# RWKV and sparse-attention steps queued behind dense work already written, and one group's element work spread wider

## The chip, the cores and the metric

One core of a Trainium2 chip runs one launch of the kernel. The metric is the device time of the launch in microseconds (us); lower is better. The engines named below are TensorE (PE in the rows; PEld is its weight load), VectorE (DVE), ScalarE (ACT), GpSimd (POOL) and SyncE (SP), which here issues most transfers.

## The reference

One decoder layer on 256 tokens of width 2048, cut to what matters:

```python
p = rms_norm(h) @ w_in                       # all input projections
y_rwkv = rwkv7_group(p[:, :RWKV_COLS])       # 16 heads x 64
#   per token: sa = S @ -kk;  S = S*w + sa (kk*a)^T + v k^T;  y = S @ r
y_att = dsa_group(p[:, RWKV_COLS:])          # indexer scores, top 64 keys of a query, attention
h = h + concat(y_rwkv, y_att) @ w_mix_out
h = h + cross_attention(rms_norm(h), rms_norm(mem))
h = h + square(relu(rms_norm(h) @ w_up)) @ w_down
return rms_norm(h)
```

## The kernel before

**Dense work.** Every large product is written as three matmuls: a float32 weight tile `raw` is loaded (`stream`, L176, SyncE's queue, four buffers), ScalarE copies it to a rounded part `whi` (L182), VectorE subtracts that from it and leaves the rest `wlo` (L183; three buffers of each), and `gemm` multiplies hi by hi, hi by lo and lo by hi: L210 to L212 in a panel of kind "B" (128x256 outputs), L222 to L224 in one of kind "A" (128x512 and 128x296), L216 and L218 in one of kind "C". I write att0#3 for the fourth weight tile of the panel whose weights are `w_att0`. The dense panels of the mixed part come in this order: a small panel, rkv0, gates, rkv1, att1 (attention keys and values), att0 (indexer queries), rkv2 and rkv3 (keys and values of RWKV group 1), ck (cross-attention keys, from `mem`), att2 (attention queries), and then mix0, mix2 and mix1, the output projection of RWKV group 0, of the attention and of RWKV group 1. From 542 us of the span on come only the rest of mix1, cross attention with its projections, and the MLP. An operand tile `xhl` of `mem` is made by `load_t` (ScalarE L311, VectorE L312), and ck's first matmuls need the first of these.

**Side work.** Beside the dense panels go three generators.
- RWKV, once for each of two groups of eight heads. `rwkv_elem` makes two arrays, AR and BK, out of r, k, the decay and the gate, for two pairs of heads at a time: matmuls L453, L468, L490, transposes L509, and on VectorE L471 to L500, L511 to L515, L519 and, last, L518. `rwkv_gram` multiplies them (L538, in four chunks of 64 tokens; L541 masks the result on VectorE), transposes BK and v (L567, L579, L588), and solves a triangular system by a substitution on VectorE (L601, L603), whose result comes back through DRAM (L617) for L631 and L639. `rwkv_state` walks the four chunks (L682 to L702), with outputs L713 and L716 and a normalisation (`norm`: L725 to L747; L740 spreads the scale with a matmul, L743 to L745 and L747 are its tail on VectorE).
- Sparse attention. `dsa_qi` and `dsa_kv` make rotary embeddings and indexer scores (L858, on VectorE L865 and L867) and find the 64 largest by eight rounds of L878 and L879; `dsa_att` is the attention.
- `shift_bank` (L347, L349, L351) mixes an RWKV projection with its neighbour in time, behind each rkv panel.

**What sets the order.** `run` merges the generators: each yields how much dense time its step should be spread over, and `run` always takes the one that is least far (`scaled` multiplies these amounts). A scheduler then works through the operations, and among those that it holds ready, what was written first goes first; it sets the order on each engine for good. On the chip each engine executes its list in that order. The two halves that matter below are `g_stream`, the dense panels, and the others: `r_group(0)`, `r_group(1)` and `d_stream`.

Of the kernel before, what the change touches and what calls it, by code (L numbers as in the profile page):

```python
# [10 lines left out]
F32 = mybir.dt.float32  # L11
# [11 lines left out]
T = 256  # L23
# [56 lines left out]
def hybrid_block(ctx: ExitStack, tc: tile.TileContext, I, out):  # L80
# [36 lines left out]

    done, now = {}, [0.0]

# [3 lines left out]
    def run(*gens):  # L123


        live = [[0.0, g, None, f] for g, f in gens]
        while live:
            ready = [e for e in live if e[2] is None or e[2] in done]
# [7 lines left out]
            try:  # L136
                r = next(e[1])
            except StopIteration:
# [35 lines left out]
    def stream(pack, i, n, hl=None):  # L174
        raw = wpool.tile([P, 1024], F32, tag="raw", bufs=NRAW, name="raw")
        last_load[:] = [nc.sync.dma_start(raw[:, :n], pack[i][:, :n])]  # L176
        if hl is None:
            hi = wop.tile([P, 1024], F32R, tag="whi", bufs=NHL, name="whi")
            lo = wop.tile([P, 1024], F32R, tag="wlo", bufs=NHL, name="wlo")
        else:  # L180
            hi, lo = hl[:, 0], hl[:, 1]
        S.activation(hi[:, :n], raw[:, :n], AF.Copy)  # L182
        V.tensor_tensor(lo[:, :n], raw[:, :n], hi[:, :n].bitcast(F32), op=ALU.subtract)  # L183
        return hi, lo

    def gemm(pack, ncol, kts, xt, blocks, nk=1, hook=None, alt=False):
# [9 lines left out]
        for chunk, k in enumerate(range(0, kts, nk)):  # L196
# [4 lines left out]
            for kind, col, w, bank, sel in blocks:  # L201
                for a in range(n):
                    first, last = k + a == 0, k + a == kts - 1
                    c0 = a * ncol + col
                    wh, wl = hi[:, c0:c0 + w], lo[:, c0:c0 + w]
                    xh, xl = operand(xt, k + a)
                    if kind == "B":
# [3 lines left out]
                        TE.matmul(o, wh, xl, start=False, stop=False, skip_group_check=True)  # L211
                        TE.matmul(o, wl, xh, start=False, stop=last, skip_group_check=True)  # L212
                    elif kind == "C":
# [3 lines left out]
                                  start=first, stop=False, skip_group_check=True)  # L217
                        TE.matmul(o[:, :T], wl, xh, start=False, stop=last, skip_group_check=True)  # L218
                    else:
# [3 lines left out]
                        TE.matmul(o, xh, wl, start=False, stop=False)  # L223
                        TE.matmul(o, xl, wh, start=False, stop=last)  # L224
            yield sum(b[2] if b[0] == "A" else T for b in blocks) * n * 3 * 0.000422
# [790 lines left out]
    def r_group(g):  # L1016
        yield f"r{g}"
        yield (10.0, 10.0)[g]
        yield from scaled(rwkv_elem(g), (0.8, 1.0)[g])
        yield from scaled(rwkv_gram(g), (0.8, 0.75)[g])  # L1020
# [293 lines left out]
```

## Time and profile before

| | us |
|---|---|
| three runs | 1352.95, 1354.51, 1358.34 |
| median | 1354.51 |
| the profiled execution | 1358.12 |
| its span, first to last instruction | 1356.3 |
| TensorE busy / VectorE busy / ScalarE busy in the span | 1318.3 / 876.3 / 684.2 |
| mean granted clock of TensorE (1.0 is 2.4 GHz) | 0.981 |

The rows further down are read in this order: busy shares, the chain that ended last, what TensorE waited for, then windows of the span with busy time and granted clock, and in the windows where clock or busy time fall short the single instructions. In a row of the timeline "[3.17 <-DVE BK L518]" says that the engine stood idle for 3.17 us before it and that the end of L518 on VectorE, writing BK, released it. A clock of 0.5 is TensorE's lower level, 1.2 GHz.

### The profile page before, as it was taken

The numbers are of one execution on the slowest core, as the hardware profiler recorded it, in microseconds if no ns is written. First come the engines' busy times: TensorE is split into PE (matmuls) and PEld (weight loads), VectorE is DVE, ScalarE is ACT, GpSimd is POOL, SyncE is SP. The second block draws the span as 40 slices with busy tenths as digits, with TensorE's granted clock in tenths as the row PEclk, the third lists the DMA queues.
The fourth block names the chain that finished last, engine by engine and source line by source line (L and its number), as shares of the span: only waits on it lengthen the run. The fifth ranks groups of instructions, "written<-read, shape, count | busy, mean of one in ns | idle before, by whom it ended". The sixth has DMA issues, their size and how long they took to land.

```text
span 1356.3 us, 20607 instructions
## 1 busy us (share of the span) xinstructions
PE 1318.3 (97%) x7989; PEld 1141.1 (84%) x7989; DVE 876.3 (65%) x1459; ACT 684.2 (50%) x1009; POOL 20.6 (2%) x69
## 2 busy tenths in 40 slices
PE   7999799997999999999999999999999999999997
PEld 7999788987978778887888888888888888888886
DVE  5477676599777765776665656555656556565655
ACT  5545334546544663666553544445445344363453
POOL 0001000001000000000000000000000000000000
PEclk9999699998899999999999999999999999999999
DMA  8844345334657425565666666666666666666663
GB/s 262 284 133 139 99 156 160 107 109 131 201 153 235 129 83 153 183 219 173 184 186 199 189 190 195 189 190 192 191 190 191 195 187 187 199 188 191 195 190 123
DMA packets 81489, 239.06 MB, mean 176 GB/s; under 512 B 20752, under 2 KB 20880, under 8 KB 81392
## 3 DMA queue, kind: packets, MB, share of 16 engines
q1 hardware_dynamic: 76864, 237.15, 57.4%
q8 instruction: 62, 1.02, 0.3%
q10 hardware_dynamic: 4528, 0.61, 0.3%
q14 instruction: 35, 0.29, 0.1%
HBM read 234.58 MB, written 3.15 MB: 175 GB/s over the span
## 4 chain that ended last, share of the span: by engine, by line
PE 85%; DMA 5%; DVE 5%; ACT 3%; issue 1%; SPq 0%; DVEq 0%; ACTq 0%; POOL 0%; POOLq 0%
PE gb L216 17%; PE gb L222 13%; PE gb L223 13%; PE gb L224 13%; PE gb L218 9%; PE gb L211 4%; PE gb L210 4%; PE gb L212 4%; DVE wlo L183 2%; ACT whi L182 1%; DMA x_tm<-in_x 1%; PE pg L538 1%; PE psi L858 1%; DMA raw<-in_w_mix 1%; DMA x_tm<-in_mem 1%
## 5 line engine op out<-in xcount | busy, mean ns | idle before, releaser
L183 DVE TENSOR_TENSOR wlo<-raw,whi 128x1024 fp32r<-128x1024 f32 (+2 forms) x416 | 498.4, 1200 | 365.5 <-ACT whi L182 362.5
L182 ACT ACTIVATE whi<-raw 128x1024 fp32r<-128x1024 f32 (+2 forms) x416 | 432.1, 1041 | 493.0 <-PE gb L224 249.5
L216 PE MATMUL gb<-xhl,whi 128*128 128x512 f32 x1024 | 350.4, 394 | 0.3 <-DVE hres L1045 0.3
L218 PE MATMUL gb<-xhl,wlo 128*128 128x256 f32 x1024 | 269.9, 279 | 0.0
L216 PEld LDWEIGHTS gb<-xhl,whi 128*128 128x128 f32 x1024 | 189.4, 188 | 38.5 <-ACT xhl L265 0.7
L218 PEld LDWEIGHTS gb<-xhl,wlo 128*128 128x128 f32 x1024 | 192.7, 188 | 6.4
L224 PE MATMUL gb<-whi,ul 128*128 128x512 f32 x480 | 186.9, 389 | 0.0
L223 PE MATMUL gb<-wlo,uh 128*128 128x512 f32 x480 | 186.9, 389 | 0.0
L210 PE MATMUL gb<-xhl,whi 128*128 128x256 f32 x560 | 163.5, 294 | 7.6 <-ACT whi L182 6.2
L211 PE MATMUL gb<-xhl,whi 128*128 128x256 f32 x560 | 163.1, 292 | 0.0
L212 PE MATMUL gb<-xhl,wlo 128*128 128x256 f32 x560 | 160.2, 291 | 2.2 <-DVE wlo L183 2.2
L222 PE MATMUL gb<-whi,uh 128*128 128x512 f32 x480 | 132.2, 389 | 0.0
L210 PEld LDWEIGHTS gb<-xhl,whi 128*128 128x128 f32 x560 | 109.8, 196 | 10.7 <-ACT whi L182 6.2
L212 PEld LDWEIGHTS gb<-xhl,wlo 128*128 128x128 f32 x560 | 109.0, 197 | 4.3 <-DVE wlo L183 2.8
L211 PEld LDWEIGHTS gb<-xhl,whi 128*128 128x128 f32 x560 | 110.2, 197 | 1.7 <-DVE xhl L312 0.9
L222 PEld LDWEIGHTS gb<-whi,uh 128*128 128x128 f32 x480 | 90.1, 188 | 18.8
L224 PEld LDWEIGHTS gb<-whi,ul 128*128 128x128 f32 x480 | 90.1, 188 | 18.7
L223 PEld LDWEIGHTS gb<-wlo,uh 128*128 128x128 f32 x480 | 90.1, 188 | 18.6
L223 PE MATMUL gb<-wlo,xhl 128*128 128x512 f32 (+1 forms) x224 | 82.5, 373 | 0.7 <-DVE wlo L183 0.6
L224 PE MATMUL gb<-whi,xhl 128*128 128x512 f32 (+1 forms) x224 | 81.9, 370 | 0.0
L222 PE MATMUL gb<-whi,xhl 128*128 128x512 f32 (+1 forms) x224 | 65.1, 376 | 0.2 <-ACT whi L182 0.2
L1045 DVE TENSOR_TENSOR hres<-hres,gb 128x512 f32<-128x512 f32 x92 | 57.4, 680 | 0.1
(390 smaller groups left out, 1425.7 us busy)
## 6 DMA issues: line engine op xcount, KB each, us to landing
raw<-in_w_up SPq DMA_DIRECT2D x128, 512.0 KB, 4.2
raw<-in_w_dn SPq DMA_DIRECT2D x128, 512.0 KB, 4.2
raw<-in_w_rkv SPq DMA_DIRECT2D x48, 512.0 KB, 3.9
raw<-in_w_att SPq DMA_DIRECT2D x32, 512.0 KB, 4.2
raw<-in_w_mix SPq DMA_DIRECT2D x32, 512.0 KB, 3.7
raw<-in_w_att SPq DMA_DIRECT2D x16, 296.0 KB, 3.1
rawx<-in_memT SPq DMA_DIRECT2D x8, 512.0 KB, 3.9
raw<-in_w_ck SPq DMA_DIRECT2D x8, 512.0 KB, 3.7
```

Of the source, the lines that this page charges most:

```text
L182: S.activation(hi[:, :n], raw[:, :n], AF.Copy)
L183: V.tensor_tensor(lo[:, :n], raw[:, :n], hi[:, :n].bitcast(F32), op=ALU.subtract)
L210: TE.matmul(o, wh, xh, start=st_, stop=False, skip_group_check=True)
L211: TE.matmul(o, wh, xl, start=False, stop=False, skip_group_check=True)
L212: TE.matmul(o, wl, xh, start=False, stop=last, skip_group_check=True)
L216: TE.matmul(o, wh, xt[(k + a) // 4][:, (k + a) % 4].rearrange("p s t -> p (s t)"), start=first, stop=False, skip_group_check=True)
L218: TE.matmul(o[:, :T], wl, xh, start=False, stop=last, skip_group_check=True)
L222: TE.matmul(o, xh, wh, start=first, stop=False)
L223: TE.matmul(o, xh, wl, start=False, stop=False)
L224: TE.matmul(o, xl, wh, start=False, stop=last)
L538: TE.matmul(pgs[e][:, j * P:j * P + P], BK[half[e], c, j].rearrange("p a t -> p (a t)"), AR[half[e], c, j].rearrange("p a t -> p (a t)"), ...
L1045: V.tensor_tensor(dst, dst, banks[b * 2 + t], op=ALU.add)
```

## The change

`run` traces every step of a generator that is not the first (so all side work) inside `behind(last["mm"])` and `behind(last["lo"])`. `behind` puts a lower bound on the order: TensorE's operations of that step come behind the dense matmul that was written last, VectorE's behind the last `wlo` split that was written. `stream` and `gemm` record these two. Nothing is bound on ScalarE, GpSimd and SyncE. The steps of `rwkv_elem(0)` yield 2.0 instead of 0.8 times their amount, so that group 0's element work, and what follows it, is merged later. `mm_chain` is defined and not called. The number of instructions stays the same on every engine, but for two ACT_TABLE_LOADs fewer on ScalarE. Lines behind the middle of the file move by 16 (L538 is L554 in the new file, L740 is L756, L183 is L199, L210 to L212 are L226 to L228, L222 to L224 are L238 to L240).

```diff
--- before.py
+++ after.py
@@ -1,5 +1,5 @@
 import math
-from contextlib import ExitStack
+from contextlib import ExitStack, nullcontext
 
 import numpy as np
 
@@ -115,7 +115,20 @@
         return pss.tile([P, 512], F32, tag="d", bufs=2, name=name)
 
 
-    done, now = {}, [0.0]
+    def behind(ins):
+
+        return tc.issue_after(ins.ins) if ins else nullcontext()
+
+    def mm_chain(calls):
+
+        prev = None
+        for a, kw in calls:
+            with behind(prev):
+                prev = TE.matmul(*a, **kw)
+
+
+
+    done, now, last = {}, [0.0], {}
 
     def mark(key):
         done[key] = now[0]
@@ -124,6 +137,7 @@
 
 
         live = [[0.0, g, None, f] for g, f in gens]
+        gen0 = gens[0][0]
         while live:
             ready = [e for e in live if e[2] is None or e[2] in done]
             assert ready, [e[2] for e in live]
@@ -134,7 +148,9 @@
             e = min(ready, key=lambda e: e[0])
             now[0] = e[0]
             try:
-                r = next(e[1])
+
+                with behind(e[1] is not gen0 and last.get("mm")), behind(e[1] is not gen0 and last.get("lo")):
+                    r = next(e[1])
             except StopIteration:
                 live.remove(e)
                 continue
@@ -179,8 +195,8 @@
             lo = wop.tile([P, 1024], F32R, tag="wlo", bufs=NHL, name="wlo")
         else:
             hi, lo = hl[:, 0], hl[:, 1]
-        S.activation(hi[:, :n], raw[:, :n], AF.Copy)
-        V.tensor_tensor(lo[:, :n], raw[:, :n], hi[:, :n].bitcast(F32), op=ALU.subtract)
+        last["hi"] = S.activation(hi[:, :n], raw[:, :n], AF.Copy)
+        last["lo"] = V.tensor_tensor(lo[:, :n], raw[:, :n], hi[:, :n].bitcast(F32), op=ALU.subtract)
         return hi, lo
 
     def gemm(pack, ncol, kts, xt, blocks, nk=1, hook=None, alt=False):
@@ -200,7 +216,7 @@
                 hook[k]()
             for kind, col, w, bank, sel in blocks:
                 for a in range(n):
-                    first, last = k + a == 0, k + a == kts - 1
+                    first, end = k + a == 0, k + a == kts - 1
                     c0 = a * ncol + col
                     wh, wl = hi[:, c0:c0 + w], lo[:, c0:c0 + w]
                     xh, xl = operand(xt, k + a)
@@ -209,19 +225,19 @@
                         st_ = first and sel == 0
                         TE.matmul(o, wh, xh, start=st_, stop=False, skip_group_check=True)
                         TE.matmul(o, wh, xl, start=False, stop=False, skip_group_check=True)
-                        TE.matmul(o, wl, xh, start=False, stop=last, skip_group_check=True)
+                        last["mm"] = TE.matmul(o, wl, xh, start=False, stop=end, skip_group_check=True)
                     elif kind == "C":
 
                         o = banks[bank]
                         TE.matmul(o, wh, xt[(k + a) // 4][:, (k + a) % 4].rearrange("p s t -> p (s t)"),
                                   start=first, stop=False, skip_group_check=True)
-                        TE.matmul(o[:, :T], wl, xh, start=False, stop=last, skip_group_check=True)
+                        TE.matmul(o[:, :T], wl, xh, start=False, stop=end, skip_group_check=True)
                     else:
                         o = banks[bank][:, :w]
                         xh, xl = xh[:, sel * P:sel * P + P], xl[:, sel * P:sel * P + P]
                         TE.matmul(o, xh, wh, start=first, stop=False)
                         TE.matmul(o, xh, wl, start=False, stop=False)
-                        TE.matmul(o, xl, wh, start=False, stop=last)
+                        last["mm"] = TE.matmul(o, xl, wh, start=False, stop=end)
             yield sum(b[2] if b[0] == "A" else T for b in blocks) * n * 3 * 0.000422
         return banks
 
@@ -1016,7 +1032,7 @@
     def r_group(g):
         yield f"r{g}"
         yield (10.0, 10.0)[g]
-        yield from scaled(rwkv_elem(g), (0.8, 1.0)[g])
+        yield from scaled(rwkv_elem(g), (2.0, 1.0)[g])
         yield from scaled(rwkv_gram(g), (0.8, 0.75)[g])
         yield from scaled(rwkv_state(g, yr), (0.6, 1.617)[g])
         mark(f"y{g}")
```

The order is the same as before on every engine up to att1#9, and again from the fourth weight tile of mix1 to the end. What happens between is seen at three places.

TensorE, where att1 ends and att0 begins; pg is a product of `rwkv_gram(0)`, gb are dense banks. Before:

```order
L224 MATMUL gb_1433<-whi,xhl 128x296
L538 MATMUL pg_1373<-AR,BK 128x128 x4
...
L538 MATMUL pg_1513<-AR,BK 128x128 x4
L567 MATMUL pb<-par,BK 128x128 x16
L579 MATMUL rb<-par,rke 128x128 x8
L588 MATMUL pv<-par,vp 128x128 x12
L222 MATMUL gb_1923<-whi,xhl 128x512
```

After:

```order
L240 MATMUL gb_1335<-whi,xhl 128x296
L525 MATMUL ss<-par,inve 128x128 x2
L554 MATMUL pg_1692<-AR,BK 128x128 x4
L554 MATMUL pg_1693<-AR,BK 128x128 x4
L238 MATMUL gb_1727<-whi,xhl 128x512
...
L240 MATMUL gb_1730<-whi,xhl 128x512
L554 MATMUL pg_1749<-AR,BK 128x128
...
L583 MATMUL pb<-par,BK 128x128 x8
...
L595 MATMUL rb<-par,rke 128x128 x8
```

The block of 68 products and transposes that stood between the two panels is spread in groups of eight and more over att0; the first eight products and two transposes (L525) still stand between the panels.

TensorE, where rkv3 (bank gb_3383) ends and ck (gb_3838, gb_3839) begins; py, pm, pvv and psdb are RWKV state 0, psi is the indexer, zw, za, sst and ss are `rwkv_elem(1)`. Before:

```order
L211 MATMUL gb_3383<-xhl,whi 128x256
L212 MATMUL gb_3383<-xhl,wlo 128x256
L509 MATMUL ss<-par,inve 128x128 x4
L210 MATMUL gb_3838<-xhl,whi 128x256
L210 MATMUL gb_3839<-xhl,whi 128x256
L453 MATMUL zw<-lx,lora 128x256 x2
L453 MATMUL za<-lx,lora 128x256 x2
L211 MATMUL gb_3838<-xhl,whi 128x256
```

After:

```order
L228 MATMUL gb_3383<-xhl,wlo 128x256
L756 MATMUL psdb<-par,sde 128x128 x2
L729 MATMUL py<-AR,Sn 64x64 x8
L732 MATMUL py<-Gm_1691,X 64x64 x8
L874 MATMUL psi<-kT,qiT 128x256 x4
L741 MATMUL pm<-y,par 128x256
...
L469 MATMUL zw<-lx,lora 128x256 x2
...
L506 MATMUL sst<-par,rkk 128x2 x2
...
L226 MATMUL gb_3838<-xhl,whi 128x256
L226 MATMUL gb_3839<-xhl,whi 128x256
L469 MATMUL zw<-lx,lora 128x256 x2
L227 MATMUL gb_3838<-xhl,whi 128x256
```

Forty-five side matmuls now follow each other between the two panels; 39 of them ran inside rkv2 and rkv3 before.

VectorE in the same place, from one split of ck's weights to the first operand tile of `mem` (xhl). After, with 49 rows left out of the middle; the next split of ck comes 15 rows behind the last one shown:

```order
L199 TENSOR_TENSOR wlo<-raw,whi 128x1024
L883 SCALAR_TENSOR_TENSOR acc<-rel,wi,acc 128x256
L759 TENSOR_TENSOR y<-y,psdb 128x256
...
L534 TENSOR_TENSOR BK<-a__3548,ss 64x4x64 x2
L894 MAX m_3437<-wk 128x8
L328 SCALAR_TENSOR_TENSOR xhl<-rawx,par,xhl 128x256
L534 TENSOR_TENSOR BK<-a__3554,ss 64x4x64 x2
L328 SCALAR_TENSOR_TENSOR xhl<-rawx,par,xhl 128x256 x2
```

Before, the corresponding piece, from the split of the same weight tile (ck#2) on:

```order
L183 TENSOR_TENSOR wlo<-raw,whi 128x1024
L515 SCALAR_TENSOR_TENSOR a__3548<-kx,hkk,a__3548 128x256
L515 SCALAR_TENSOR_TENSOR a__3554<-kx,hkk,a__3554 128x256
L879 MATCH_REPLACE wk<-m_3437,wk 128x256
L518 TENSOR_TENSOR BK<-a__3548,ss 64x4x64 x2
L518 TENSOR_TENSOR BK<-a__3554,ss 64x4x64 x2
L312 SCALAR_TENSOR_TENSOR xhl<-rawx,par,xhl 128x256
L878 MAX m_3440<-wk 128x8
L312 SCALAR_TENSOR_TENSOR xhl<-rawx,par,xhl 128x256 x5
```

The split of ck#2 and the first operand tile of `mem` had five rows between them and have 53 rows of RWKV, indexer and shift work between them now.

TensorE, from the end of mix2 (banks gb_5702 to gb_5705) into mix1 (gb_5854 on), whose operands yh and yl are what RWKV state 1 ends with; psdb is that state's last chunk. Before:

```order
L223 MATMUL gb_5703<-wlo,oh 128x512
L740 MATMUL psdb<-par,sde 128x128 x2
L224 MATMUL gb_5703<-whi,ol 128x512
...
L223 MATMUL gb_5705<-wlo,oh 128x512
L224 MATMUL gb_5705<-whi,ol 128x512
L222 MATMUL gb_5854<-whi,yh 128x512
L223 MATMUL gb_5854<-wlo,yh 128x512
```

After:

```order
L240 MATMUL gb_5705<-whi,ol 128x512
L747 MATMUL pvv<-par,ysq 128x2 x2
L238 MATMUL gb_5854<-whi,yh 128x512
...
L239 MATMUL gb_5854<-wlo,yh 128x512
L240 MATMUL gb_5854<-whi,yl 128x512
L756 MATMUL psdb<-par,sde 128x128 x2
L238 MATMUL gb_5855<-whi,yh 128x512
```

The last L740 stood 29 dense matmuls ahead of mix1 and now stands nine matmuls behind its first.

## Rows read from the trace of the kernel before

**Rows 1.** Page, busy time of each engine: us, share of the span, instructions

```profile
PE 1318.3 (97%) x7989; PEld 1141.1 (84%) x7989; DVE 876.3 (65%) x1459; ACT 684.2 (50%) x1009; POOL 20.6 (2%) x69
```

**Rows 2.** Page, the chain that ended last, shares by engine

```profile
PE 85%; DMA 5%; DVE 5%; ACT 3%; issue 1%; SPq 0%; DVEq 0%; ACTq 0%; POOL 0%; POOLq 0%
```

**Rows 3.** What TensorE waited for: us in total, times, longest

```profile
PE zw L453 <- DVE BK L518: 5.5, 1, 5.5
PE pg L538 <- DVE BK L518: 3.6, 2, 3.2
```

**Rows 4.** Windows: length, busy us of PE, PEld, DVE, ACT, POOL, clock, DMA, GB/s

```profile
141.00:179.00 38.00, 31.75 (x148) 27.53 (x147) 23.13 (x56) 12.46 (x24) 2.56 (x9) 0.69 0.27 75
179.00:216.00 37.00, 37.00 (x222) 30.28 (x222) 27.81 (x56) 15.85 (x17) 0.90 (x2) 1.00 0.72 211
326.00:390.00 64.00, 56.30 (x363) 50.70 (x362) 48.47 (x111) 32.53 (x67) 4.19 (x11) 0.84 0.51 153
328.60:338.90 10.30, 7.06 (x28) 6.16 (x28) 9.55 (x26) 4.75 (x13) 0.81 (x2) 0.50 0.43 118
542.00:1356.00 814.00, 803.93 (x4158) 685.51 (x4156) 491.72 (x605) 406.81 (x543) 0.00 (x0) 1.00 0.62 188
```

**Rows 5.** TensorE timeline where att1 ends: start, us, engine, line, operation, [wait]

```profile
140.86 0.30 PE L224 MATMUL gb<-whi,xhl 128*128 128x296 f32 x1
144.32 12.79 PE L538 MATMUL pg<-AR,BK 64*128 64x128 f32 x64 [3.17 <-DVE BK L518]
...
167.47 0.78 PE L222 MATMUL gb<-whi,xhl 128*128 128x512 f32 x1
```

**Rows 6.** VectorE timeline there

```profile
144.21 0.87 DVE L518 TENSOR_TENSOR BK<-a__1210,ss 64x256 f32<-64x256 f32 x2
```

**Rows 7.** TensorE timeline: att0#3, substitution, first of rkv2

```profile
178.59 0.84 PE L222 MATMUL gb<-whi,xhl 128*128 128x512 f32 x3
...
213.77 1.19 PE L631 MATMUL p<-ut,Gm 32*32 32x32 f32 x62
...
215.69 0.28 PE L210 MATMUL gb<-xhl,whi 128*128 128x256 f32 x1
```

**Rows 8.** TensorE timeline, products of RWKV group 1, low and full clock

```profile
356.38 2.12 PE L538 MATMUL pg<-AR,BK 64*128 64x128 f32 x16 [0.40 <-DVE BK L518]
...
369.86 1.49 PE L538 MATMUL pg<-AR,BK 64*128 64x128 f32 x16
```

**Rows 9.** Lines of TensorE, 106 to 390 us: busy us, mean ns, idle before

```profile
L858 PE MATMUL psi<-kT,qiT 64*128 64x256 f32 x32 | 6.8, 402 | 0.0
```

**Rows 10.** TensorE timeline, from rkv3 into ck

```profile
323.52 0.38 PE L509 MATMUL ss<-par,inve 128*128 128x128 f32 x2
...
331.84 1.19 PE L453 MATMUL zw<-lx,lora 64*128 64x256 f32 x2 [5.50 <-DVE BK L518]
...
334.70 0.58 PE L211 MATMUL gb<-xhl,whi 128*128 128x256 f32 x1
```

**Rows 11.** VectorE timeline, operand tiles of mem

```profile
333.35 2.20 DVE L312 SCALAR_TENSOR_TENSOR xhl<-rawx,par,xhl 128x256 fp32r<-128x256 f32 x5
```

**Rows 12.** Lines of VectorE, 216 to 335 us: busy us, mean ns, idle before

```profile
L867 DVE SCALAR_TENSOR_TENSOR acc<-rel,wi,acc 128x128 f32<-128x128 f32 (+1 forms) x30 | 12.4, 413 | 1.3 <-ACT rel L861 0.5
L878 DVE MAX8 m<-wk 128x8 f32<-128x128 f32 (+1 forms) x16 | 5.7, 355 | 0.2
L879 DVE MATCH_REPLACE8 wk<-m,wk 128x128 f32<-128x128 f32 (+1 forms) x15 | 5.1, 338 | 0.0
...
L743 DVE TENSOR_TENSOR y<-y,psdb 128x256 f32<-128x256 f32 x4 | 1.7, 418 | 0.8 <-PE psdb L740 0.8
```

**Rows 13.** Page, groups: the copy to whi on ScalarE

```profile
L182 ACT ACTIVATE whi<-raw 128x1024 fp32r<-128x1024 f32 (+2 forms) x416 | 432.1, 1041 | 493.0 <-PE gb L224 249.5
```

**Rows 14.** TensorE and VectorE timelines, end of RWKV state 1

```profile
525.68 0.38 PE L740 MATMUL psdb<-par,sde 128*128 128x128 f32 x2
...
529.54 0.42 DVE L747 TENSOR_TENSOR yl<-y,yh 128x256 fp32r<-128x256 f32 x1
```

## The prediction

> **What bounds the kernel now.** The busy shares come first: TensorE works 1318.3 us, VectorE 876.3 and ScalarE less [rows 1], and the chain that ended last is 85% TensorE and only 5% each for transfers and VectorE [rows 2]. So a change of order can win only what TensorE loses to waits and to its lower clock, and it loses wherever it makes new waits. The list of waits then shows that two of TensorE's three longest have one releaser, the last VectorE operation of `rwkv_elem`, L518: 5.5 us in front of L453 and 3.2 of 3.6 in front of L538 [rows 3]. The windows say where this is. From 542 us to the end the clock is 1.00 and TensorE is busy 803.93 of 814, in an order that the change leaves alone. From 179 to 216 it is busy every microsecond. Two windows fall short: 141 to 179 (busy 31.75 of 38, clock 0.69) and 326 to 390 (56.30 of 64, clock 0.84) [rows 4]. The first is the product block of RWKV group 0, the second the start of ck and the products of group 1.
>
> In the first, the timeline shows att1 ending at 141.15, a wait of 3.17 us until the second L518 pair has ended near 144.3, and then 64 records of L538 that take 12.79 us; att0 begins only at 167.47 [rows 5, 6]. Sixteen of these records take 2.12 us at the lower clock and 1.49 at the higher [rows 8]. So the block costs a wait, a slow stretch behind it, and then another wait and another slow stretch.
>
> **Gram of group 0: a gain of about 6.4 us.** I sum up what att0 and the block would take at full clock. From att0#3 to rkv2#0 are 37.1 us, of which L631 takes some 1.4 (some of it inside att0#15) [rows 7], so 35.7 for 13 weight tiles, 2.74 each; 16 tiles are 43.5 or a little more. The block: 64 records of L538 at 1.49 per sixteen [rows 8], 6.0, a little more where they stand in small groups, 7.1 together; transposes L567, L579 and L588, 36 short ones, 4.6 at the higher clock. An alternation of dense and side work costs about 0.13 us (my estimate: sums of single pitches with that amount give the lengths of rkv2 and rkv3 of this trace to within 0.3 us); there are 18, so 2.3. Total 57.5 us. Before, the same work went from 141.15 to 214.3 (215.69 less the 1.4), 73.2 us: 15.7 more.
>
> Not all of that comes back, for in the new order ten side operations still stand between att1's last matmul and att0's first, and the eight L538 among them need the last L518. On VectorE behind the split of att1's last tile now stand L515, L492, L511, L513, L514, two L519, a split, two L518, L515, two splits and two L518, about 8 us, where 6 stood before the end at 145.08 [rows 6]; it begins some 2 us earlier, because the element step itself was moved behind. I get 145.4 to 146 for the last L518, hence a wait of about 4.3 us without cover. The clock fell after 3.17 us of waiting here [rows 4, 5], so I let it fall again: a slow stretch of 10 us, as the one from 328.6 to 338.9 at clock 0.50 [rows 4], which costs half of it where TensorE works it through, 4.7. So att0 ends at 141.15 + 4.3 + 57.5 + 4.7 = 207.7, rounded 208, against 214.3. The bounds: no fall of the clock, 203; a second fall as before, 213.
>
> The Trainium skill, Perfetto Trace Analysis, section Optimization Strategy, says that where the most contended engine changes over time, interleaving those regimes may improve performance. By that rule the wait and the slow stretch would both be covered and the 15.7 us be won entirely. The row that speaks against it is the wait in front of L538, whose releaser stays ahead of att0 in the new order.
>
> **rkv2 and rkv3: shorter, because work leaves them.** From 214.3 to the end of rkv3 at 323.5 [rows 10] TensorE works almost without a gap, 109.2 us. The state steps now begin nine tiles later (the substitution begins at att0#10 instead of ahead of att0), and 39 matmuls leave this stretch: six L858 (0.40 each by their mean [rows 9]), ten L453, L468 and L490, and 23 of normalisation and outputs, which I put at 6 us together since most are small; that and a dozen alternations at 0.13 less is near 9, +- 2, while four L588 come in at 0.4. So the end of rkv3, T, is 208 + 109.2 + 0.4 - 9.0 = 308.6, instead of 323.5.
>
> **Start of ck: the 15 us are lost again, and 5 more.** This is the place that decides. Before, ck's first full matmuls began at 334.70, after 5.50 us of waiting and a slow stretch [rows 3, 10]. They need two operand tiles of `mem`, the first two L312 (the second begins at 333.35 [rows 11]). In the new order VectorE must first make the split of ck#2, and that needs the third `whi` and `wlo` buffer, which rkv3's last tile frees at T; ScalarE's copy takes 1.04 [rows 13], the split 1.2. Whatever VectorE has finished by then, it waits there for T, since its list is executed in order. Behind this split stand 53 rows before the first L312, two more to the second. In us, by [rows 12]: eleven L867 at 0.40 (4.4), seven rounds of L878 and six of L879 with its load (4.6), two chunks of normalisation, ten operations near 0.4 with two short ones (3.2), four L351 and two L347 (3.0), the second pair of `rwkv_elem(1)` from L482 to L518 (9.2) and the two L312 (0.8): 25.2. All of it is work that was spread over rkv3 before, where it hid behind dense matmuls. Beside that, five steps of this list wait for TensorE and ScalarE in turn (the scale of the normalisation through L740, sst through L468 and L490, the transposed ss through L509), each for the other engines' latency. The nearest rows: four L743 waited 0.8 for L740 [rows 12], the first L538 0.40 for L518 [rows 8], and L453 5.50 [rows 3, 10]; several engines pass the work on in each step, so I take 0.8 for each, 4 in all. So ck goes on at 308.6 + 1.0 + 1.2 + 25.2 + 4 = 340.0, that is 5.3 later than before; 45 side matmuls, about 9 us, run in that time with no dense work between them, so TensorE idles for about 20 us where it idled and crawled for about 10. The bounds: without any of the 4, 336; with a T of 313 and 8 us of such waits, 348.
>
> **Products of group 1.** From the second L312 to the first L538 of group 1 passed 23.0 us (333.35 to 356.38 [rows 8, 11]), filled by VectorE. The rows between them are nearly the same in the new order, 24.0 by the same prices: L538 at 364.3, later by 7.9. TensorE has only a few ck tiles as cover there, as before, and I leave the stalls and the slow stretch around it as they were.
>
> **The entry into mix1: 2.3 us.** The last L740 of RWKV state 1 stood 29 dense matmuls, some 6.7 us, ahead of mix1, and its tail on VectorE, the last L747, ended at 529.96 [rows 14], behind which 3 us of dense work were still to come. Now it stands nine matmuls behind mix1's first, and the next bank needs its result. What is left uncovered is the way from L740 to L747: three VectorE operations at 0.42, a ScalarE copy and L747, 2 to 2.5 us. The bounds: nothing, if the scheduler's slack is larger than I see, and 3.9 (525.68 to 529.54 plus its last operation).
>
> **Edits that I cost at nothing.** Two table loads fewer on ScalarE, which works for half of the span [rows 1], so a gain there moves no end; and the 814 us from 542 on, with the same order as before [rows 4].
>
> **Sum.** 7.9 + 2.3 = +10.2 us against the trace's own 1358.1 (span 1356.3), and the same difference against the median, which the profiled execution exceeds by 3.6: 1354.5 + 10.2 = 1364.7, rounded 1365.
>
> **The rivals.**
> - Faster. VectorE is done with its backlog when T comes. For it: it is busy 876 of 1356 us [rows 1], and ran ahead easily from 179 to 216 (27.81 of 37 [rows 4]). Then ck starts shortly after T. With no fall of the clock at att0 (T 304) and half of the 25 us done ahead, ck goes on at 304 + 2.2 + 12.6 + 4 = 322.8 and the products come at 346.8, 9.6 earlier than before; with mix1's entry that is 1347. With two thirds done ahead it is 1343. Against it: the list on VectorE is fixed, the split of ck#2 stands ahead of the 53 rows, and its buffer is not free before T. By the rule of the Trainium skill cited above (Perfetto Trace Analysis), with the 15.7 us won and kept to the end, the time would be 1354.5 - 15.7 = 1339; the wait that stays ahead of att0 leaves it 0.02 of this case's 0.12.
> - About the same. The clock does not fall at att0, so T is 304, and the five steps pass each other without waits: ck goes on at 304 + 27.4 = 331.4, the products come at 355.4, 1.0 earlier than before, and mix1's entry costs 0 to 2.3. That is 1353 to 1356, and 1358 with half of the waits.
> - Much slower. The clock falls in the 20 us in which only small matmuls run, so that the chain from TensorE to VectorE and back is slower at each hop, T slips to 313 (a second fall at att0) and the five steps cost 8 to 12 us: ck goes on at 348 to 352, the products come at 372 to 376, and with mix1's entry that is 1373 to 1378. It decides from the point at which T is late by 4 and the steps cost 8. For it: after 5.50 us of waiting the first matmuls of ck ran at half clock until 338.9.
> - The bound on the order does nothing at these places. Against it: the order printed above has changed.
>
> **How the numbers follow.** Forecast, slower by 7 to 15 us: 0.41. Much slower: 0.20. About the same: 0.27. Faster: 0.12. A measurement of this kernel tells half a per cent, 6.8 us, from no change: the bounds are 1347.7 and 1361.3. So slower has 0.61, same 0.27, faster 0.12. The range for 8 in 10 leaves out 0.1 on either side: the faster case below 1344, and of the much slower one what lies above its prices; 1344 to 1381. The forecast alone lies between 1361 and 1370.
>
> **What would show it right or wrong.** Right: the first product of group 0 waits 3 to 5 us behind att1 at a clock that falls, and the rest stand inside att0 at full clock; att0 ends near 208 and rkv3 near 309; then VectorE does not pause for some 25 us while TensorE idles for about 20, with ck's L227 (the old L211) at 340 and the first product of group 1 near 364; and a wait of 2 us stands a few matmuls into mix1. Wrong: if ck starts within 10 us of rkv3's end, the VectorE list was not behind the split when it mattered, and the faster case holds; if the lengths of rkv2 and rkv3 do not shrink by 8 us or more, the substitution's later start has a price that I have not seen; and if anything changes behind 600 us, the argument from the equal order is wrong.

## The result, and the profile after

The changed kernel takes 1369.51 us (median; 1367.19 to 1372.65) against 1353.73 for the kernel before: a ratio of 1.0099, 95% interval 1.0081 to 1.0118. That is slower by some 13 us by the ratio; the two medians lie 15.8 apart, still inside the interval. 10 were forecast, and 1365 as the time. The profiled execution took 1371.2 us, its span is 1369.4, 13.1 more than before.

The page of the changed kernel has nearly the same busy times as [rows 1]; TensorE's 1321.7 is 3.4 more, the rest of the 13 us is waiting:

```profile
span 1369.4 us, 20598 instructions
PE 1321.7 (97%) x7989; PEld 1139.3 (83%) x7989; DVE 875.8 (64%) x1459; ACT 679.8 (50%) x1007; POOL 21.8 (2%) x69
```

TensorE's waits (us in total, times, longest). The 5.5 in front of L453 of [rows 3] is 3.2 now, and a row of new ones stands beside it, nearly all between a few side operations of TensorE, VectorE and ScalarE:

```profile
PE pg L554 <- DVE BK L534: 7.7, 3, 3.3
...
PE psdb L756 <- ACT sde L752: 3.7, 2, 1.9
PE zw L469 <- DVE BK L534: 3.2, 1, 3.2
...
PE ss L525 <- DVE rk L508: 2.7, 1, 2.7
...
PE gb L238 <- ACT yh L762: 1.9, 1, 1.9
PE sst L506 <- DVE rkk L500: 1.6, 1, 1.6
PE sst L484 <- ACT lw L474: 1.4, 1, 1.4
```

Windows of the changed kernel (columns as in [rows 4]). The first is the window that had clock 0.69 before. The next two run from the end of rkv3 to the first ck block and on to the first product of group 1, then the stretch up to att2#3, and the entry into mix1:

```profile
141.00:179.00 38.00, 34.17 (x174) 27.71 (x175) 20.27 (x26) 10.96 (x14) 0.00 (x0) 0.87 0.44 134
...
304.80:335.00 30.20, 17.10 (x88) 12.43 (x88) 27.23 (x75) 15.95 (x35) 4.21 (x12) 0.60 0.11 36
335.00:362.00 27.00, 23.69 (x167) 22.35 (x166) 23.31 (x54) 16.83 (x37) 2.09 (x6) 0.88 0.59 183
362.00:399.70 37.70, 36.22 (x189) 30.08 (x190) 16.56 (x36) 12.91 (x22) 1.39 (x5) 0.77 0.40 114
541.40:554.60 13.20, 10.61 (x40) 7.93 (x41) 5.58 (x11) 4.00 (x6) 0.00 (x0) 0.87 0.29 79
```

In the 30 us behind rkv3 VectorE works 27.23 us and TensorE 17.10, much of it at half clock. That is the place the prediction named.

Where each trace stands at eleven places, in us from the span's start, read from the start of TensorE's first matmul there (for "end of rkv3", the end of its last one; for ck, the first L211 or L227):

| | before | after | difference |
|---|---|---|---|
| end of att1 | 141.2 | 140.3 | -0.9 |
| first of rkv2 | 215.7 | 203.6 | -12.1 |
| end of rkv3 | 323.7 | 304.8 | -18.9 |
| ck goes on | 334.7 | 335.0 | +0.3 |
| first product of group 1 | 356.4 | 362.0 | +5.6 |
| att2#3 | 390.1 | 399.7 | +9.6 |
| mix0 | 426.4 | 437.5 | +11.1 |
| mix2 | 463.6 | 471.7 | +8.1 |
| mix1 | 533.1 | 541.4 | +8.3 |
| mix1#3 | 541.5 | 554.6 | +13.0 |
| end of TensorE's work | 1348.1 | 1361.1 | +13.1 |

So 19 us are won by the end of rkv3 (0.9 of them already at the end of att1), all of them are gone when ck goes on, 9 more are lost up to att2#3, and 4.7 at mix1. From mix1#3 to the end both kernels take the same time.

TensorE's timeline at the first gain, the end of att1: two waits for L534 (L518 before), then the second group of products at full clock inside att0:

```profile
142.60 0.90 PE L554 MATMUL pg<-AR,BK 64*128 64x128 f32 x6 [2.12 <-DVE BK L534]
145.74 2.59 PE L554 MATMUL pg<-AR,BK 64*128 64x128 f32 x10 [2.23 <-DVE BK L534]
...
156.32 1.16 PE L554 MATMUL pg<-AR,BK 64*128 64x128 f32 x16
```

VectorE's timeline at ck: the split of ck#2, and, 27 us after the split's end, the second operand tile of `mem`, the first of the pair at 334.74:

```profile
306.36 1.23 DVE L199 TENSOR_TENSOR wlo<-raw,whi 128x1024 fp32r<-128x1024 f32 x1 [1.09 <-ACT whi L198]
307.50 0.48 DVE L883 SCALAR_TENSOR_TENSOR acc<-rel,wi,acc 128x256 f32<-128x256 f32 x1
...
333.36 0.47 DVE L328 SCALAR_TENSOR_TENSOR xhl<-rawx,par,xhl 128x256 fp32r<-128x256 f32 x1
333.86 0.85 DVE L534 TENSOR_TENSOR BK<-a__3554,ss 64x256 f32<-64x256 f32 x2
334.74 0.88 DVE L328 SCALAR_TENSOR_TENSOR xhl<-rawx,par,xhl 128x256 fp32r<-128x256 f32 x2
```

On TensorE the last wait ahead of ck is not for an operand tile but for the L534 that ends 0.4 us before the first of them begins; L227 then follows L469 without a pause. Both stand at the end of the same piece of VectorE's list:

```profile
333.04 2.07 PE L469 MATMUL zw<-lx,lora 64*128 64x256 f32 x4 [3.23 <-DVE BK L534]
335.04 0.58 PE L227 MATMUL gb<-xhl,whi 128*128 128x256 f32 x1
```

And TensorE at mix1: the last L756 (L740 before), nine matmuls in, and the next bank 1.88 us behind it, at 0.6 us a matmul in place of 0.4, the mark of the lower clock:

```profile
544.28 0.39 PE L240 MATMUL gb<-whi,yl 128*128 128x512 f32 x1
544.51 0.40 PE L756 MATMUL psdb<-par,sde 128*128 128x128 f32 x2
546.79 0.79 PE L238 MATMUL gb<-whi,yh 128*128 128x512 f32 x1 [1.88 <-ACT yh L762]
547.38 0.63 PE L239 MATMUL gb<-wlo,yh 128*128 128x512 f32 x1
```

### The profile page after: what moved, and what is told of

The parts are those of the page before. It is cut to its first block, busy times and chain, and to the rows that moved or that the text cites. A ratio compares the mean times of both kernels' runs of the same rounds, so it can differ in the third digit from the quotient of the medians.

```text
span 1369.4 us, 20598 instructions
## 1 busy us (share of the span) xinstructions
PE 1321.7 (97%) x7989; PEld 1139.3 (83%) x7989; DVE 875.8 (64%) x1459; ACT 679.8 (50%) x1007; POOL 21.8 (2%) x69
## 4 chain that ended last, share of the span: by engine, by line
PE 85%; DVE 7%; DMA 5%; ACT 2%; issue 1%; DVEq 0%; ACTq 0%; SPq 0%
PE gb L232 17%; PE gb L239 13%; PE gb L238 13%; PE gb L240 13%; PE gb L234 9%; PE gb L227 3%; PE gb L226 3%; PE gb L228 3%; DVE wlo L199 2%; DMA raw<-in_w_rkv 2%; ACT whi L198 1%; PE pg L554 1%; DMA raw<-in_w_ck 1%; PE psi L874 1%; PE gb L1148 1%
## 5 line engine op out<-in xcount | busy, mean ns | idle before, releaser
L199 DVE TENSOR_TENSOR wlo<-raw,whi 128x1024 fp32r<-128x1024 f32 (+2 forms) x416 | 498.3, 1200 | 371.8 <-ACT whi L198 368.9
L240 PE MATMUL gb<-whi,ul 128*128 128x512 f32 x480 | 186.9, 389 | 0.0
L226 PE MATMUL gb<-xhl,whi 128*128 128x256 f32 x560 | 162.9, 293 | 7.7 <-ACT whi L198 6.7
L228 PE MATMUL gb<-xhl,wlo 128*128 128x256 f32 x560 | 159.8, 291 | 2.9 <-DVE wlo L199 2.9
L227 PE MATMUL gb<-xhl,whi 128*128 128x256 f32 x560 | 162.1, 291 | 0.0
L238 PE MATMUL gb<-whi,uh 128*128 128x512 f32 x480 | 132.2, 389 | 0.0
L226 PEld LDWEIGHTS gb<-xhl,whi 128*128 128x128 f32 x560 | 109.3, 196 | 10.8 <-ACT whi L198 6.9
L228 PEld LDWEIGHTS gb<-xhl,wlo 128*128 128x128 f32 x560 | 108.0, 195 | 5.1 <-DVE wlo L199 4.0
L227 PEld LDWEIGHTS gb<-xhl,whi 128*128 128x128 f32 x560 | 109.3, 195 | 3.0 <-issue 1.1
L238 PEld LDWEIGHTS gb<-whi,uh 128*128 128x128 f32 x480 | 90.1, 188 | 18.8
L240 PEld LDWEIGHTS gb<-whi,ul 128*128 128x128 f32 x480 | 90.1, 188 | 18.7
L240 PE MATMUL gb<-whi,xhl 128*128 128x512 f32 (+1 forms) x224 | 82.6, 374 | 0.0
L238 PE MATMUL gb<-whi,xhl 128*128 128x512 f32 (+1 forms) x224 | 69.0, 378 | 0.2 <-ACT whi L198 0.2
```

The costliest lines, as they stand in the source:

```text
L199: last["lo"] = V.tensor_tensor(lo[:, :n], raw[:, :n], hi[:, :n].bitcast(F32), op=ALU.subtract)
L226: TE.matmul(o, wh, xh, start=st_, stop=False, skip_group_check=True)
L228: last["mm"] = TE.matmul(o, wl, xh, start=False, stop=end, skip_group_check=True)
L238: TE.matmul(o, xh, wh, start=first, stop=False)
L240: last["mm"] = TE.matmul(o, xl, wh, start=False, stop=end)
```

## The experiments

**First question: which part of the change does it?** My theory (A) was that the later element work makes both the gain at att0 and the loss at ck, and the bound little. The rival (B) was that the bound makes the loss. Four kernels take the change apart. The edits, all of the changed kernel, are those of `spread_only`, `te_only` and `bound_only`, in this order; `ve_only` keeps the other `behind`:

```diff
-                with behind(e[1] is not gen0 and last.get("mm")), behind(e[1] is not gen0 and last.get("lo")):
+                with nullcontext():
```

```diff
-                with behind(e[1] is not gen0 and last.get("mm")), behind(e[1] is not gen0 and last.get("lo")):
+                with behind(e[1] is not gen0 and last.get("mm")):
```

```diff
-        yield from scaled(rwkv_elem(g), (2.0, 1.0)[g])
+        yield from scaled(rwkv_elem(g), (0.8, 1.0)[g])
```

> Only the factor 2.0 of the element work of group 0 is kept, no step is bound behind dense work. Theory A (the later element work makes the loss, the bound little): the order still has L538 spread over att0, 20.8 us of VectorE work (by the prices of the trace of before) between the split of ck#2 and the first operand tile of mem instead of 23.8, and the last L740 of state 1 behind mix1's first matmuls; so att0 ends near 204, ck goes on some 3 us earlier than in the changed kernel, mix1 waits as there: 1362 to 1368. Theory B (the bound makes the loss, by holding side work until dense work has been written): ck and mix1 come in time, the gain at att0 stays: 1343 to 1350.

Measured: 1367.99, ratio 1.0099 (1.0069 to 1.0129), the same as the whole change. ck goes on 0.5 us earlier than in the changed kernel, where 3 were expected.

> Only the bound is kept, the factor goes back to 0.8. Theory A: the product block of group 0 stands whole between att1 and att0 as before (no gain there), 7.6 us of VectorE work stand ahead of the first mem tile instead of 3.3, and the last L740 stands behind mix1's first matmuls: 4 us lost at ck, 4 to 5 at mix1, 1358 to 1364. Theory B: the loss of the changed kernel without its gain at att0, 1370 or more.

Measured: 1358.98, ratio 1.0018 (0.9999 to 1.0038). B falls with these two: without the bound the loss is all there, and with the bound alone nearly nothing is left of it. The bound costs or gives what the order happens to become with it: its two halves alone, in the next two runs, lie below and above the whole change.

> Factor 2.0, and the bound on TensorE alone. The order has the same spread block, 25.6 us of VectorE work ahead of the first mem tile, but the last L740 of state 1 in mix2 again, 29 dense matmuls ahead of mix1. Theory A: the 4.8 us of the changed kernel at mix1 are gone, ck is as late or 2 us later: 1363 to 1368. Theory B: no clear difference from the changed kernel, 1367 to 1373.

Measured: 1364.55, ratio 1.0068 (1.0043 to 1.0093), as theory A had it.

> Factor 2.0, and the bound on VectorE alone. The order has 18.1 us of VectorE work ahead of the first mem tile and the last L740 behind mix1's first matmuls. Theory A: ck goes on 5 us earlier than in the changed kernel, mix1 waits as there: 1360 to 1366. Theory B: the bound that holds VectorE's work back is the one that counts, so as the changed kernel, 1367 to 1373.

Measured: 1379.38, ratio 1.0166 (1.0123 to 1.0210); neither theory had it so high. rkv3 ends only at 318.7, and ck goes on 6 us later than in the changed kernel, where 5 earlier were expected. Its single executions run from 1371 to 1384, and their mean granted clocks from 0.982 to 0.970. The trace is of the slowest; it has 34 us at half clock behind a wait of 3.61 us in front of the products of group 1. Windows of `ve_only`:

```profile
346.00:366.50 20.50, 17.89 (x145) 17.13 (x143) 15.57 (x30) 14.22 (x30) 1.97 (x5) 1.00 0.50 163
366.50:400.60 34.10, 31.52 (x119) 26.58 (x120) 13.76 (x29) 6.86 (x10) 1.38 (x5) 0.50 0.32 100
```

The traces of these kernels, laid side by side, give two of the prediction's terms by themselves. The second column is the VectorE work, summed by prices of the trace of before, that each order puts between the split of ck#2 and the first operand tile of `mem`; the third is the time from the end of rkv3 until ck goes on; the last is the time from mix1's first matmul to mix1#3, and before it where the last L740 stands.

| kernel | VectorE work ahead, us | end of rkv3 to ck, us | last L740 | entry into mix1, us |
|---|---|---|---|---|
| before | 3.3 | 11.0 | in mix2 | 8.4 |
| bound_only | 7.6 | 12.8 | in mix1 | 13.3 |
| ve_only | 18.1 | 22.3 | in mix1 | 14.6 |
| spread_only | 20.8 | 25.6 | in mix1 | 13.2 |
| after | 23.8 | 30.3 | in mix1 | 13.2 |
| te_only | 25.6 | 32.9 | in mix2 | 8.4 |

The time until ck goes on follows the VectorE work ahead of it, with 4 to 8 us on top in each. Counted from the span's start it hardly moves: ck goes on between 332.2 and 335.2 in five of these kernels, and at 341.0 in ve_only, while the end of rkv3 lies anywhere between 302.2 and 323.7. So what TensorE wins before, it waits away there. And the entry into mix1 costs 8.4 us where L740 comes ahead of it, 13.2 or more where it does not. In `te_only` L756 ends 7 us ahead of mix1, and the wait is gone:

```profile
531.77 0.38 PE L756 MATMUL psdb<-par,sde 128*128 128x128 f32 x2
...
539.18 0.47 PE L238 MATMUL gb<-whi,yh 128*128 128x512 f32 x1 [0.43 <-DVE hres L1061]
```

**Second question: is the place of the `mem` operands what loses the 19 us?** If so, making them earlier should keep the gain. The edit, with four tiles (early3 has three; before_early4 makes it in the kernel before, spread_early4 in spread_only):

```diff
         elif name == "v1":
+            for q in range(4): load_t("memT", "g_mem", mt0, 4 * q)
             yield from rkv_panel(3)
...
-        load_t("memT", "g_mem", mt, 0)
+        if not mt: load_t("memT", "g_mem", mt, 0)
...
-        mt = []
+        mt = mt0
...
```

> The changed kernel, but three of the four operand tiles of mem are loaded and split ahead of rkv3 instead of at ck, so ck's first matmuls no longer stand behind VectorE's pile of side work; the pile is then cut up by the splits of ck's weights. The last L740 stands behind mix1's first matmuls as in the changed kernel. Theory A (the place of the mem operands behind the pile makes the loss at ck): ck goes on within 5 us of rkv3's end, near 308, a part of the gain comes back as a wait ahead of group 1's products, which need the same VectorE work, and mix1 still waits: 1344 to 1355. Rival C (VectorE's work in sum sets when att2 can go on, whatever ck does): group 1's products come at 362 as in the changed kernel and everything behind them too, 1363 to 1370.

Measured: 1373.51, ratio 1.0122 (1.0103 to 1.0141), above the ranges of both theories; the last section shows its 51 us at half clock.

> As early3 with all four operand tiles ahead of rkv3. The order then has the products of group 1 in one block behind att2#2, and the last L740 of state 1 in mix2 again, ahead of mix1. Theory A: ck near 308, a wait ahead of the block, no wait at mix1: 1338 to 1348, below both kernels. Rival C: as the changed kernel less 5 us at mix1, 1358 to 1365.

Measured: 1362.80, ratio 1.0054 (1.0034 to 1.0074).

> Control: the kernel before with all four operand tiles of mem ahead of rkv3 and nothing else. No gain at att0; the wait of 5.5 us ahead of ck's L453 and the slow stretch behind it go; the last L740 comes behind mix1's first matmuls, which costs 4.8 as in the runs so far. Theory A: 1348 to 1355. Rival C: 1357 to 1362.

Measured: 1358.34, ratio 1.0009 (0.9995 to 1.0023), which can't be told from no change. In its trace mix1 begins 3.0 us earlier than in the kernel before; the entry into mix1, with the last L740 now behind its first matmuls, costs 13.2 instead of 8.4.

> As early4 without the bound, so only the factor 2.0 and the early operands. Theory A (the bound matters little): within 4 us of early4. Theory B (the bound matters): 6 us or more from it.

Measured: 1362.85, ratio 1.0042 (1.0027 to 1.0058); the bound matters little here too.

The first half of theory A held and the second fell. In early3 and early4 ck begins at 304.6, straight behind rkv3, 30 us earlier than before. But the first product of group 1 then comes at 366.8 and 372.2, later than in the changed kernel, and att2#3 at 402.3 and 395.0. Up to mix1#3 early4's trace is 8.8 us ahead of the changed kernel's: 4.7 of that at mix1's entry, since the last L740 is in mix2 again, and 4.1 ahead of it. Windows of early4 from the end of rkv3 on; TensorE is busy while ck lasts, and in the next 29 us it works 14:

```profile
304.20:343.00 38.80, 36.32 (x283) 31.93 (x281) 33.83 (x83) 20.15 (x38) 2.68 (x12) 1.00 0.34 109
343.00:372.20 29.20, 14.27 (x49) 11.34 (x49) 22.92 (x63) 17.03 (x37) 2.77 (x11) 0.62 0.42 127
372.20:395.00 22.80, 22.58 (x123) 20.05 (x123) 11.68 (x28) 5.42 (x9) 0.00 (x0) 0.67 0.17 35
```

The waits are the same as in the changed kernel, for L534, L508 and ScalarE's lw, only ck is no longer behind them. So the wait went to the next place where TensorE's list needs group 1's element work, as rival C said. C had the products at 362 still; that they come 5 to 10 us later it did not say.

**Third question: can the products of group 1 wait without TensorE?** They stand ahead of most of att2 in TensorE's list. With a larger factor for group 1's element work they come later in it (here in early4; 1.3 in the second kernel, and 2.0 in before_early4 for the third):

```diff
-        yield from scaled(rwkv_elem(g), (2.0, 1.0)[g])
+        yield from scaled(rwkv_elem(g), (2.0, 2.0)[g])
```

> early4 with the element steps of group 1 merged later too (factor 2.0 instead of 1.0). In the order the products of group 1 stand in four groups behind att2#3, #6, #8 and #10 instead of in one block behind att2#2, and its state ends behind mix1's first matmuls, with the last two chunks at the end of mix2. Theory D (in the changed kernel and in early4 TensorE stands idle because the products of group 1 are ahead of att2 in its list while VectorE is not done with their operands): att2#3 starts near 345 to 355 instead of 395, most of the waits between 330 and 390 go, and some come back ahead of mix1, because state 1 is late: 1342 to 1356. Rival C (VectorE's sum of work holds att2 itself): att2#3 near 390 again, 1358 or more.

Measured: 1379.04, ratio 1.0185 (1.0162 to 1.0208).

> As early4_e1_2p0 with factor 1.3. The first eight products stand behind att2#2, the others between att2#4 and #7; state 1 ends behind mix1's first matmuls. Theory D: one wait ahead of the first products remains, so att2#3 at 375 to 385, and less is lost ahead of mix1 than with 2.0: 1348 to 1360. Rival C: 1358 or more, as early4 and 5 more at mix1.

Measured: 1375.92, ratio 1.0159 (1.0140 to 1.0178).

> before_early4 with factor 2.0 for the element steps of group 1, no bound, and group 0 as in the kernel before. The products of group 1 stand in groups behind att2#2 and #5, the last L740 behind mix1's first matmuls. Theory D: ck runs without a wait, the products wait less than in before_early4 because the mem work is done, state 1 ends 5 us late at mix1: 1350 to 1358. Rival C: 1358 to 1364.

Measured: 1360.05, ratio 1.0043 (1.0026 to 1.0061).

In all three att2#3 comes earlier than in the kernel before, at 378.4, 382.1 and 379.1 instead of 390.1, where early4 was 4.8 later and before_early4 0.8 earlier. That is no gain yet: the products now stand behind att2#3, so less work is done by then. At mix0 the three are at 426.4, 430.6 and 421.6, against 426.4 before. And the waits did not go, as theory D had it: between 330 and 390 us TensorE works 42.4 us in early4, 42.8 in early4_e1_2p0 and 42.8 in early4_e1_1p3 (some 17 us of pauses in each). In the last two, 13 and 14 us of these stand in front of other steps of group 1's element work (L525, L469, L484), which the factor left ahead of att2#3. In early4_e1_2p0 the state of group 1 is late; mix1 begins at 539.3, 6 us later than in the kernel before, and the way to mix1#3 takes 20.6 us in place of 8.4, with the last L756 of state 1 and its matmuls in a chain of waits:

```profile
543.12 0.44 PE L756 MATMUL psdb<-par,sde 128*128 128x128 f32 x2 [1.01 <-ACT sde L752]
545.71 0.70 PE L741 MATMUL pm<-y,par 128*128 128x256 f32 x2 [0.92 <-ACT y L735]
...
548.56 0.44 PE L756 MATMUL psdb<-par,sde 128*128 128x128 f32 x2 [1.07 <-ACT sde L752]
550.88 0.80 PE L238 MATMUL gb<-whi,yh 128*128 128x512 f32 x1 [1.88 <-ACT yh L762]
```

Theory D fell: of the ranges that I expected by it, 1342 to 1356, 1348 to 1360 and 1350 to 1358, none was met; its place for att2#3 was right for the second kernel (375 to 385) and wrong for the first (345 to 355, and 378.4 in the trace). before_early4_e1_2p0 came out in rival C's range. The other two fit C's "1358 or more", which is open upwards; neither had a chain of 20 us at mix1.

**Last question: VectorE's work or the waits between the engines?** The work up to the first product of group 1 is the same in both kernels. VectorE is the third busy column of these two windows, from 100 us to that product, of before and then of after:

```profile
100.00:356.40 256.40, 241.66 (x1893) 217.17 (x1892) 193.70 (x449) 127.02 (x218) 16.40 (x49) 0.93 0.45 135
```

```profile
100.00:362.00 262.00, 239.98 (x1896) 213.67 (x1894) 193.30 (x450) 125.88 (x219) 17.06 (x48) 0.92 0.44 133
```

193.70 and 193.30 us, with 63 and 69 us of pauses. Behind the end of rkv3 the kernel before has this (the changed kernel's two windows, 304.80 to 362.00, stand in the first section):

```profile
323.50:356.40 32.90, 25.23 (x179) 23.69 (x177) 31.39 (x75) 20.91 (x45) 3.35 (x8) 0.84 0.56 174
```

So VectorE pauses 1.5 us there before and 6.7 after, where 50.5 of 57.2 us are work. Ahead of the end of rkv3 that leaves 162.3 us of work in 223.5 us before, and 142.8 in 204.8 after: 61 and 62 us of pauses. The stretch became 19 us shorter, VectorE's pauses in it did not, and so 19.5 us of its work were left over for the time behind rkv3. To tell the work from the waits there, some of the work is left out:

```diff
-            for _ in range(NSEL // 8):
+            for _ in range(NSEL // 8 if t == 0 else 1):
```

> The changed kernel with seven of the eight rounds of L894 and L895 (max and replace, L878 and L879 of the kernel before) left out for the second half of the queries, so some 5 us of VectorE work less behind the end of rkv3; the selection of keys is then another. In the order 21.5 us stand ahead of the second operand tile of mem instead of 23.8, and the last L740 is in mix2 again. Theory E (behind rkv3's end VectorE's sum of work sets when group 1's products come): ck goes on 2 us earlier, the first product 5 us earlier, near 357, and with 4.8 us less at mix1 1357 to 1362. Rival F (the waits between the engines set it, not the work): the first product stays at 361 to 362, and only mix1's 4.8 us are gone: 1363 to 1366.

Measured: 1359.03, ratio 1.0033 (1.0015 to 1.0052). The window of this kernel from 100 us to its first product:

```profile
100.00:355.70 255.70, 239.22 (x1883) 214.03 (x1881) 187.48 (x428) 124.54 (x216) 15.88 (x49) 0.92 0.43 133
```

5.8 us of VectorE work less, and the product comes 6.3 us earlier; att2#3 comes 8.4 earlier, and mix1 is entered in 8.5 us again. The time lies in theory E's range and the product near where E had it: behind rkv3 it is VectorE's work that holds TensorE up. How much each microsecond of that work is worth is not settled by it. The operands of the products (L534) are ready at 352.7 instead of 362.0, more than the work left out, ck goes on 3.9 us earlier where 2 were expected, and the product no longer waits at all, where it waited 3.3. The order shifted with the edit, so single places can't be compared to better than a few microseconds.

What the change gains on TensorE before, VectorE has not gained: since 100 us it must do its 193 us, and its pauses do not shrink with att0. The largest part of these pauses stands in front of the dense panels' own splits: from 100 us to the end of rkv3, 33.7 us before and 35.9 after in front of L183 and L199, waiting for ScalarE's copy to `whi`; and ScalarE's waits in front of that copy (50 us before, 58 after) end with a dense matmul of TensorE. So VectorE's side work stands in one list with splits that go at the pace of the dense panels. This is read from the waits; no run here moves the splits, so what the side work would gain by it is open.

No version that I ran is faster than the kernel before.

## Why the prediction was right, and where not

**The sign and the place.** The time, 1369.5, lies in the range, 4.5 above the forecast. The gain at att0, its full loss at ck, the further loss at group 1's products and the wait at mix1 were all there.

**Gram of group 0.** The wait without cover was 2.12 + 2.23 = 4.35, forecast 4.3. The clock fell, as forecast. att0 ended at 203.6, not 208: the term for the block, 14.0 with its alternations, was too large. In the trace of after sixteen records of products inside att0 take 1.10 us until the next dense matmul (156.32 to 157.42), alternation included, eight transposes 0.8; the whole block comes to some 9 us at full clock. By the measure of the forecast (from att1's end, without L631, which the changed kernel runs inside rkv2) the stretch took 63.3 us in place of 73.2: the gain was 9.9 where 6.4 was forecast. att0's end lies near the bound "no fall of the clock", 203, in spite of the fall.

**rkv2 and rkv3.** They took 304.8 - 203.6 = 101.2; 100.6 was forecast.

**Start of ck.** The split of ck#2 began 1.6 us behind rkv3's end, at 306.36; 1.0 was forecast. From its end to the second L328, 307.6 to 335.2, VectorE took 27.6 us, 25.9 of work and 1.8 of waits; 25.2 and 4 were forecast. ck went on at 335.0, 30.3 behind T, and after an interruption by four more L469 at 338.6; 31.4 was forecast. TensorE's idle time was smaller than the 20 us I gave, 13.1 (30.20 less 17.10), because its side work ran at the lower clock. That part of the rival "much slower" came true: half clock from 314 to 342, longer than the slow stretch of [rows 4].

But the reading behind this term was too narrow. I took the place of the `mem` operands for the cause. It is only the first place where VectorE's backlog is waited for: with ck freed (early4) only 4 us were won beside mix1's 4.7.

**Products of group 1.** They came at 362.0, +5.6; +7.9 was forecast. (340.0 and the 24.0 give 364.0, +7.6, by the forecast's own terms; it has 364.3.) ck was 5.0 earlier than forecast, mostly from the block's price above, and from the second L328 (334.74) 27.3 us passed instead of 24.0. "I leave the stalls and the slow stretch around it as they were" failed: from there to att2#3 the trace of after takes 37.7 us at clock 0.77, where before took 33.7 (356.4 to 390.1), 4.0 more. A wait of 1.49 us for a split at att2#4 adds 1.5, and 3.0 are given back between mix0 and mix2, which I have not traced.

**The entry into mix1.** This is the mis-sized term: 2.3 forecast, 4.8 measured (13.2 against 8.4). The wait from L756 to yh is 1.88, as priced. I left out that a split ahead of it comes late too (0.71) and that the clock falls once more, which costs 1.7 in 3.4 us. My upper bound of 3.9 did not hold it, nor does 4.3, which it comes to with the last operation that it names.

**The sum.** +7.9 to mix1 and +2.3 were forecast, +8.3 and +4.7 are in the trace. That the first agrees is luck, by errors of opposite sign: the products were 2.3 earlier than forecast, the stretches behind them 2.5 longer (4.0 + 1.5 - 3.0).

**The Trainium skill's rule** (Perfetto Trace Analysis, Optimization Strategy, on interleaving regimes with different contended engines) was borne out in its own stage, in part: the block interleaved with att0 gave 9.9 of the 15.7 us there. By that rule alone the time would have been 1339; the next stage, whose contended engine is VectorE, took it back.

## What to carry to other kernels

Time won on the busiest engine in one stage lasts only as far as the next place where another engine's list must be at a given step; so before counting a gain, sum that other engine's work up to that place, and see whether the change shortens that work or the pauses in it. A reordering is priced by what it puts ahead of the next dense operation's last operand: here the time until ck went on followed that sum over six kernels. And where a move makes something late at the end of a stage, the lower clock behind a wait belongs into the price, since here it cost about as much as the wait.

## What the runs showed of the hardware

The lower clock could cost as much as the waits in front of it, and more. In early3 a chain of waits of 0.8 to 4.8 us, with small side matmuls between, left TensorE at clock 0.50 for 51 us, in which it was busy 33.8: by half of the busy time, an estimate, the clock cost 17 us there and the waits 17. The window of early3:

```profile
333.30:384.50 51.20, 33.77 (x130) 28.05 (x130) 34.67 (x91) 22.30 (x50) 3.21 (x13) 0.50 0.26 76
```

In `ve_only` it stayed at 0.50 for 34.1 us although TensorE was busy 31.52 of them, behind one wait of 3.61 and one of 1.58, and without a pause from 370.7 on: 16 us by the same estimate, against 5 of waits. In the changed kernel the clock was back after 10 us behind the waits at att0 (143.7 to 153.9). I had counted a slow stretch as 10 us; 3.4 to 51 are in these traces, and I can't tell beforehand which.
